# Splitting a feed-forward half between two expert stages, with its rows kept in DRAM

## The chip, the core and the metric

The kernel runs on one core of a Trainium2 chip. The metric is the device time of one execution in microseconds (us). Of the engines, PE (TensorE) multiplies, DVE, ACT and POOL work on vectors, and SP issues nearly all loads, in the order of one queue; 16 DMA engines move the data.

## The reference

Two blocks of two layers follow each other. The first takes the tokens x [256, 1024]; the second takes its output and a context ctx [256, 1024] of its own:

```python
# first block, layer i = 0, 1
h = h + (forgetting_attention if i == 0 else retention)(rms_norm(h), ...)
h = h + hier_moe(rms_norm(h), ...)         # 32 experts, two per token
# second block, layer l = 0, 1
mod, modc = silu(c) @ w_mod[l] + b_mod[l], silu(c_ctx) @ w_mod[l] + b_mod[l]   # six vectors of 1024 each
x  = x  + g1 * (mix(x, xc) @ w_out[l])     # needs the states of the context's mixer
x  = x  + g2 * swiglu(rmsnorm(x, norm2_g[l]) * (1 + sc2) + sh2, w_gu[l], w_down[l])
if l == 0:
    xc = xc + gc1 * (mix_c(xc) @ w_out[0])
    xc = xc + gc2 * swiglu(rmsnorm(xc, norm2_g[0]) * (1 + scc2) + shc2, w_gu[0], w_down[0])
```

The context's half of the second block does not depend on the first block. It is mixer, feed-forward half, and then of layer 1 only the part of the mixer that gives the states. The feed-forward half has 2816 hidden units.

## The kernel before

**Stages.** `run` (L1755) traces the main path: fox (the attention), moe(0), retention, moe(1), and then the second block's tokens. Beside each of the first four stages stands "side" work that does not depend on it. `weave` (L1737) traces a ratio R0 to R3 of side steps for each step of the main path, and what is left when the main path ends follows it (`drain`). The place in the trace becomes the place in each engine's order, save for the few pieces that a raised priority puts ahead. The side work is:

- beside fox, `early`: small vectors, then `mods(0, (0, 1))`
- beside moe(0): the context's `mixer(0, 1)`
- beside retention, `later`: `mods(0, (2,))`, the set-up of layer 1, `mods(1, (0,))`
- beside moe(1), `ctx`: the context's `ffn(0, 1)` and then `mixer(1, 1, full=False)`

**mods** (L1191) makes a third (or more) of the six modulation vectors: for each third eight loads of w_mod of 1 MB, each with four products of 128 x 512 (L1211), which appear as eight MATMUL rows since a product in f32 takes two passes.

**moe** (L846). Routing: transposes (L824), logits (L828), the choice of experts on DVE, ranks (L868 to L870), a gather of tokens by products with a one-hot matrix (L895). Then eight quads q of four experts. For each of eight k a pair of 1 MB tiles of expert_w_gu (`wload2`, L153) and 16 products of 32 rows (L956); four pairs of expert_w_down with L976; the result goes to the tokens through L986 and L988. A quad has six main steps, so 48 in all. In the last quad w_down comes as sixteen half tiles (L1010).

**ffn** (L1396) of the context, in plain f32 (mode "f"). `normed2` makes the normalised rows, transposed, as a tile xt [128, 2048] of 1 MB: scale and shift rows by products (L1241), vector work (L306 is its last step), transposes (L266). Then 11 steps r. Each has a gate half and an up half (`fs`, L416: one load of w_gu, 1 MB in rows of 1 KB, and 16 products, L430, 32 MATMUL rows) and a down part (one load of w_down of 1 MB, eight products, L1416); the down part of a step is traced after the halves of the next one.

**Weight tiles.** All loads go through one pool of six tiles of 1 MB; a load waits on SP until its tile is free, and all loads behind it on the queue wait too. At the start of moe three more tiles (`self.extra`: e0, e1, e2) lie in places that are idle then. e2 is also the place of xt in the context's halves.

Of the kernel before, what the change touches and what calls it, by code (L numbers as in the profile page):

```python
# [8 lines left out]
F32 = mybir.dt.float32  # L9
# [4 lines left out]
ALU = mybir.AluOpType  # L14
# [3 lines left out]
D, T, P = 1024, 256, 128  # L18
EPS = 1e-6
NEG = -1e30  # L20
RS = -8192.0                    # what rsqrt's scaled form carries
NE, CAP, FF = 32, 32, 512
R0, R1, R2, R3, R4 = 1.8, 0.8, 1.0, 0.88, 0.7           # steps of other work per step of the main path
AHEAD = 200                     # instructions that what the others wait for goes ahead of
TAPS = 6                        # convolution taps between other work
PIECE, WS = 512, 6              # elements per partition split at a time; pieces on chip
# [3 lines left out]
# columns of the constant array  # L30
C_ID, C_LE, C_LT, C_GE, C_ONE = 0, 128, 256, 384, 512
C_Z, C_LOW, C_UP = 640, 768, 896          # 0 where col <= row / col >= row, else NEG
C_IOTA, C_GRP, C_I8 = 1024, 1056, 1088
C_SEL, C_OFF = 1096, 1112                 # row 32 j + i, column i; rows of scales: what to add, 1 / RS
C_COS, C_SIN, C_RET = 1116, 1372, 1628         # rotary, decay
NCST = C_RET + 4 * 384

# modulation vectors: which third of the columns of w_mod, and which two of its quarters
# [4 lines left out]
def constants():  # L43
    """Tables that depend on shapes alone."""
# [35 lines left out]
class Tags:  # L80
    """A pool, some of whose tags lie in another one under other names."""
# [10 lines left out]
class Net:  # L92
    def __init__(self, tc, I, out, es):
# [10 lines left out]
        self.early, self.hold = -99, None                  # pieces of weights whose low parts GpSimd makes  # L104

# [7 lines left out]
    def bank(self):  # L113
        """One bank, from the other pool while g's are taken."""
        return self.m()[:, 0:512] if self.taken else self.g()

    def two(self, mode, apart=False):
        """Two banks."""
# [7 lines left out]
    def wt(self, name):  # L126
        """A weight tile; some lie in the places of tiles that are no longer needed."""
# [4 lines left out]
    def wload(self, src):  # L132
        """One tile of weights: rows (k p) of src on the partitions."""
# [6 lines left out]
    def wtile(self):  # L140
        """A weight tile as [P, 2, D]."""
        return self.wt("w").rearrange("p (b d) -> p b d", b=2)

    def gain(self, src, g):
        """src [D] on all partitions."""
# [3 lines left out]
    def wload2(self, src):  # L149
        """The same rows of two experts: src [2, P, 1024]."""  # L150
# [16 lines left out]
    def affine(self, o, i, scale, bias=None, eng=None):  # L167
        """o = i * scale + bias, per partition."""
# [1669 lines left out]
```

## Time and profile before

| what | value |
|---|---|
| three runs, us | 2347.91, 2349.80, 2354.22 |
| median, us | 2349.8 |
| profiled execution: span from first to last instruction, us | 2346.0 |
| mean granted clock of TensorE, share of full speed | 0.970 |
| busy share of the span: PE, DVE, ACT | 91%, 45%, 30% |
| DMA: mean rate | 293 GB/s |

The page gives no time of the profiled execution other than its span, which is 3.8 us less than the median of the runs. The stages follow from the first and last instructions of each in the timeline: fox to about 205 us, moe(0) to 770, retention to 995, moe(1) to 1632, then the second block's tokens. A view by windows gives, for each stretch, every engine's busy time, the granted clock, the busy share of the DMA engines (it can show a little over 1) and the rate in GB/s.

### The profile page before, as it was taken

What the parts mean: (1) busy time and instruction counts of PE and PEld (TensorE: products, weight loads), DVE (VectorE), ACT (ScalarE), POOL (GpSimd) and SP (SyncE); (2) the same over time, 40 slices, a digit from 0 to 9 for tenths busy, and PEclk for the clock granted to TensorE, in tenths of its full rate; (3) what the DMA queues carried; (4) which work ended last, traced back from release to release, by engine and by line L of the source; (5) the groups of instructions that cost most, each with busy time, mean ns of one, the idle gap of its engine ahead of it and who ended that gap; (6) DMA issues with size and microseconds to landing.
All of it is one profiled execution on the core that took longest, in us unless ns stands there. A gap on an engine that the chain in (4) does not pass through costs nothing. (4 is left out here: it accounts for less than half of the span.)

```text
span 2346.0 us, 32803 instructions
## 1 busy us (share of the span) xinstructions
PE 2127.2 (91%) x12844; PEld 1433.4 (61%) x12845; DVE 1060.9 (45%) x2513; ACT 695.6 (30%) x1420; POOL 172.9 (7%) x194
## 2 busy tenths in 40 slices
PE   8998899889877999989899999987998998998998
PEld 7765445344222776855444444334787997787997
DVE  6556053322101766531121221415778556777555
ACT  4353111211000434520000000012555554554554
POOL 1001000000000111010000000001212002102000
PEclk9999999999988999989999999999999999999999
DMA  8864999999999977579999999999756554555551
GB/s 257 313 245 166 350 399 392 369 399 378 379 409 384 323 281 246 203 268 382 391 398 393 399 390 390 367 356 346 256 162 202 188 190 156 187 181 171 192 185 63
DMA packets 305320, 686.64 MB, mean 293 GB/s; under 512 B 22056, under 2 KB 163784, under 8 KB 298888
## 3 DMA queue, kind: packets, MB, share of 16 engines
q1 hardware_dynamic: 305096, 684.45, 79.9%
q8 instruction: 103, 1.69, 0.3%
q14 instruction: 57, 0.47, 0.1%
q10 hardware_dynamic: 64, 0.03, 0.0%
HBM read 681.78 MB, written 2.62 MB: 292 GB/s over the span
## 5 line engine op out<-in xcount | busy, mean ns | idle before, releaser
L190 DVE TENSOR_TENSOR wl<-w,wh 128x512 fp32r<-128x512 f32 x574 | 396.3, 707 | 252.4 <-ACT wh L185 233.7
L185 ACT CAST wh<-w 128x512 fp32r<-128x512 f32 x600 | 364.3, 621 | 355.5 <-PE psm L430 111.6
L956 PE MATMUL psm<-w,xg 128*32 128x512 f32 x2048 | 319.8, 632 | 61.8 <-DMA w<-in_expert_w_gu_dram 55.0
L430 PE MATMUL psg<-xt,w 128*128 128x256 f32 x1056 | 235.8, 381 | 20.5 <-DMA w<-in_w_gu_dram 11.3
L430 PEld LDWEIGHTS psg<-xt,w 128*128 128x128 f32 x1056 | 198.0, 190 | 71.1 <-issue 38.6
L956 PEld LDWEIGHTS psm<-w,xg 128*32 128x32 f32 x2048 | 66.4, 112 | 270.6 <-issue 150.4
L430 PE MATMUL psg<-xh,wh 128*128 128x256 f32 x608 | 177.2, 291 | 3.9 <-ACT wh L185 2.4
L430 PE MATMUL psm<-xh,wh 128*128 128x256 f32 x640 | 179.9, 281 | 0.6 <-ACT ffh L1450 0.6
L430 PE MATMUL psm<-xh,wl 128*128 128x256 f32 x640 | 179.8, 281 | 0.0
L430 PE MATMUL psm<-xl,wh 128*128 128x256 f32 x640 | 179.7, 281 | 0.0
L430 PE MATMUL psg<-xh,wl 128*128 128x256 f32 x608 | 175.1, 288 | 2.4 <-DVE wl L190 2.4
L430 PE MATMUL psg<-xl,wh 128*128 128x256 f32 x608 | 173.8, 286 | 0.0
L976 PE MATMUL psm<-w,hT 128*32 128x512 f32 (+1 forms) x1152 | 156.7, 564 | 16.0 <-DMA w<-in_expert_w_down_dram 12.5
L430 PEld LDWEIGHTS psg<-xh,wh 128*128 128x128 f32 x608 | 118.1, 194 | 18.6 <-ACT wh L185 9.5
L430 PEld LDWEIGHTS psm<-xh,wh 128*128 128x128 f32 x640 | 120.7, 189 | 1.9 <-ACT ffh L1450 1.1
L430 PEld LDWEIGHTS psm<-xh,wl 128*128 128x128 f32 x640 | 120.6, 188 | 0.7
L430 PEld LDWEIGHTS psg<-xh,wl 128*128 128x128 f32 x608 | 118.0, 194 | 4.9 <-DVE wl L190 4.2
L430 PEld LDWEIGHTS psm<-xl,wh 128*128 128x128 f32 x640 | 120.8, 189 | 0.0
L430 PEld LDWEIGHTS psg<-xl,wh 128*128 128x128 f32 x608 | 117.9, 194 | 0.3 <-issue 0.2
L965 ACT ACTIVATE ha<-psm 128x512 f32<-128x512 f32 x16 | 9.6, 597 | 334.3 <-PE psm L956 334.3
L988 DVE TENSOR_TENSOR x<-x,psg 128x512 f32<-128x512 f32 (+1 forms) x72 | 45.1, 628 | 123.2 <-PE psg L986 123.0
L976 PEld LDWEIGHTS psm<-w,hT 128*32 128x32 f32 x1152 | 38.6, 111 | 93.2 <-issue 52.2
(497 smaller groups left out, 3263.9 us busy)
## 6 DMA issues: line engine op xcount, KB each, us to landing
w<-in_expert_w_gu_dram SPq DMA_DIRECT2D x256, 1024.0 KB
w<-in_expert_w_down_dram SPq DMA_DIRECT2D x112, 1024.0 KB
w<-in_w_gu_dram SPq DMA_DIRECT2D x66, 1024.0 KB
w<-in_w_mod_dram SPq DMA_DIRECT2D x48, 1024.0 KB
w<-in_w_in_dram SPq DMA_DIRECT2D x40, 1024.0 KB
w<-in_w_down_dram SPq DMA_DIRECT2D x33, 1024.0 KB
w<-in_ret_w_in_dram SPq DMA_DIRECT2D x24, 1024.0 KB
w<-in_fox_w_in_dram SPq DMA_DIRECT2D x16, 1024.0 KB
```

The source lines that it names most:

```text
L185: nc.scalar.copy(h, src)
L190: eng.tensor_tensor(l, src, h.bitcast(F32), op=ALU.subtract)
L430: self.nc.tensor.matmul(o, a, x, start=i == 0, stop=i == len(mm) - 1)
L956: nc.tensor.matmul(gu[32 * j:32 * j + 32, half * 512:(half + 1) * 512], xg[:, k, 32 * j:32 * j + 32], ws[j // 2][:, j % 2, half * 512:(hal ...
L965: nc.scalar.activation(ha, gu[:, 0:512], AF.Silu)
L976: nc.tensor.matmul(o[32 * j:32 * j + 32, :], hT[:, k, 32 * j:32 * j + 32], w(j), start=k == 0, stop=k == 3)
L988: v.tensor_tensor(o, o, ps, op=ALU.add)
```

## The change

- The modulation vectors of layer 0 are made wholly beside fox; the third that stood beside retention is gone from there.
- The context's feed-forward half is cut in two. Steps r = 0 to 3 (`SHARE = 4`) follow the mixer beside moe(0). xt is written to a DRAM buffer `keep` by a DMA on SP, and read back into its place e2 by a DMA on SP for the second part. Steps 4 to 10 stay beside moe(1). The vector g2 is made once in each part.
- One side step, the gate half of step 4, is traced ahead of moe(1), so ahead of the second routing.
- e2 is in use then, and the second moe has two extra tiles in place of three.
- The ratios are 2.4, 0.82, 0.6, 0.66 in place of 1.8, 0.8, 1.0, 0.88.

```diff
-R0, R1, R2, R3, R4 = 1.8, 0.8, 1.0, 0.88, 0.7
+R0, R1, R2, R3, R4 = 2.4, 0.82, 0.6, 0.66, 0.7
+SHARE = 4
...
     def moe(self, l):
-            self.extra = ["e0", "e1", "e2"]
+            self.extra = ["e0", "e1"] if l else ["e0", "e1", "e2"]
...
-    def ffn(self, l, i, mode, bp, b2):
+    def ffn(self, l, i, mode, bp, b2, r0=0, nr=FFN // 256, keep=None):
...
-        xin = self.normed2(l, 2, i, bp, x, mode)
+        if r0:
+            xt = bp.tile([P, 8, T], F32, tag="xt", name="xt")
+            nc.sync.dma_start(xt.rearrange("p k t -> p (k t)"), keep)
+            xin = [xt]
+        else:
+            xin = self.normed2(l, 2, i, bp, x, mode)
+        if keep is not None and not r0:
+            nc.sync.dma_start(keep, xin[0].rearrange("p k t -> p (k t)"))
...
-        nr = FFN // 256
...
-        for r in range(nr):
+        for r in range(r0, nr):
...
-            if r == 0:
+            if r == r0:
                 g2 = self.row(l, "g2", i, bp.tile([P, D], F32, tag="kt", name="g2"), mode)
...
     def run(self):
         def early():
-            yield from self.mods(0, (0, 1))
+            yield from self.mods(0)
         def later():
-            yield from self.mods(0, (2,))
             yield from self.setup_layer(1)
             yield from self.mods(1, (0,))
+        def ctx0(bp, b2):
+            yield from self.mixer(0, 1, "f", bp, b2)
+            yield from self.ffn(0, 1, "f", bp, b2, 0, SHARE, keep)
+        keep = self.dp.tile([P, 8 * T], F32, name="keep")
...
-                side = self.mixer(0, 1, "f", bp, b2)
+                side = ctx0(bp, b2)
...
             def ctx():
-                yield from self.ffn(0, 1, "f", bp, b2)
+                yield from self.ffn(0, 1, "f", bp, b2, SHARE, keep=keep)
                 yield from self.mixer(1, 1, "f", bp, b2, full=False)
             side = ctx()
+            next(side)
             self.weave(self.moe(1), side, R3)
```

Line numbers of the changed kernel are one higher up to moe, and two to eight higher behind it.

How instructions move, at three places. First PE at the second routing. Before, the last products of retention (L1165, with the split weights wh, wl and rows yh, yl) are followed by the routing's transposes of x:

```order
L1165 MATMUL psg<-wl,yh 128x512
L824 MATMUL psg<-cst,x 128x128 x8
L828 MATMUL psg<-wr,xT 128x40 x8
L868 MATMUL psg<-M,cst 128x32
L895 MATMUL psg<-oh,xn 128x128 x6
```

With the change:

```order
L1166 MATMUL psg<-wl,yh 128x512
L431 MATMUL psg<-xt,w 128x256 x16
L825 MATMUL psg<-cst,x 128x128 x8
L829 MATMUL psg<-wr,xT 128x40 x8
L869 MATMUL psg<-M,cst 128x32
```

The gate half's 16 products (L431) stand between retention's last product and the routing.

Second, SP at the same place. Before, these loads stand between retention's last weights and the last load ahead of the first wait on the routing's counts (cnti); in is w_gu of the second block, expert_w_gu of the first:

```order
L137 DMA w<-in_ret_w_out_dram 128x4x512 x7
L153 DMA w<-in_expert_w_gu_dram 128x2x1024 x7
L137 DMA w<-in_w_gu_dram 128x8x256
L1024 TENSOR_LOAD cnti
```

With the change:

```order
L138 DMA w<-in_ret_w_out_dram 128x4x512 x6
L154 DMA w<-in_expert_w_gu_dram 128x2x1024 x2
L138 DMA w<-in_w_gu_dram 128x8x256
L154 DMA w<-in_expert_w_gu_dram 128x2x1024 x5
L154 DMA w<-in_expert_w_gu_dram 128x2x1024
L1025 TENSOR_LOAD cnti
```

Eight tiles of the experts in place of seven stand ahead of the counts, and the load of w_gu two places behind retention's last.

Third, SP in moe(0) at the write of keep, with the change:

```order
L138 DMA w<-in_w_out_dram 128x4x512 x2
L154 DMA w<-in_expert_w_gu_dram 128x2x1024 x4
L138 DMA w<-in_w_gu_dram 128x8x256
L154 DMA w<-in_expert_w_gu_dram 128x2x1024 x4
L1409 DMA keep<-xt 128x2048
L138 DMA w<-in_w_gu_dram 128x8x256
```

The write of xt to keep stands behind the first load of the feed-forward half and ahead of the second; where it stands, only loads of the experts were before.

## Rows read from the trace of the kernel before

**Rows 1.** The view by windows, one row for each stage; columns stand in its head.

```profile
core 0: us, PE busy (x) PEld busy (x) DVE busy (x) ACT busy (x) POOL busy (x), PEclk, DMA share, GB/s
205.00:770.00 565.00, 476.45 (x2681) 214.94 (x2682) 141.78 (x419) 75.99 (x171) 17.76 (x30) 0.95 0.98 376
770.00:995.00 225.00, 222.22 (x1220) 174.06 (x1220) 152.32 (x321) 98.67 (x176) 28.43 (x27) 1.00 0.74 262
995.00:1632.00 637.00, 581.12 (x3145) 306.32 (x3143) 171.78 (x414) 59.94 (x136) 22.92 (x31) 0.98 0.98 371
```

**Rows 2.** The same view by 50 us: fox, moe(0), moe(1).

```profile
50.00:100.00 50.00, 48.70 (x314) 35.60 (x314) 29.11 (x75) 18.34 (x41) 0.53 (x1) 1.00 0.77 274
...
650.00:700.00 50.00, 36.59 (x198) 10.25 (x198) 2.52 (x6) 2.65 (x6) 0.00 (x0) 0.90 1.02 409
...
1250.00:1300.00 50.00, 48.33 (x252) 26.69 (x251) 10.83 (x18) 1.84 (x4) 0.76 (x2) 1.00 1.03 395
```

**Rows 3.** What PE waited for in moe(0), 217 to 770 us: total, times, longest.

```profile
PE psm L956 <- DMA w<-in_expert_w_gu_dram: 43.2, 40, 2.6
```

**Rows 4.** The same for moe(1), 1017 to 1632 us.

```profile
PE psm L956 <- DMA w<-in_expert_w_gu_dram: 11.8, 15, 1.6
```

**Rows 5.** DMA view, 730 to 770 us: rate in 40 slices of 1 us.

```profile
GB/s 410 406 401 422 410 406 401 414 418 401 390 366 351 347 346 349 350 346 348 348 347 351 346 348 353 341 347 350 347 348 347 350 346 350 346 350 345 399 388 418
```

**Rows 6.** Groups by line on PE, 0 to 205 us (fox): busy us, mean ns, idle before.

```profile
L1211 PE MATMUL psg<-w,ccol 128*32 128x512 f32 x128 | 19.1, 601 | 0.0
```

**Rows 7.** The same group, 770 to 995 us (retention).

```profile
L1211 PE MATMUL psg<-w,ccol 128*32 128x512 f32 x128 | 17.9, 604 | 0.0
```

**Rows 8.** What ACT waited for in fox, 0 to 205 us.

```profile
ACT wh L185 <- DMA w<-in_fox_w_in_dram: 10.3, 3, 6.1
```

**Rows 9.** Timeline of PE, 560 to 612 us (moe(0)): start, duration, operation.

```profile
593.08 13.97 PE L1390 MATMUL psg<-w,yT 128*128 128x512 f32 x32 [0.89 <-DMA w<-in_w_out_dram]
606.98 4.49 PE L956 MATMUL psm<-w,xg 128*32 128x512 f32 x36
```

**Rows 10.** DMA view, 570 to 612 us: rate in 40 slices of 1.05 us.

```profile
GB/s 414 406 406 410 417 410 117 23 172 339 410 355 382 390 394 423 314 398 406 396 390 402 414 400 421 410 406 406 410 417 398 414 417 254 39 27 140 312 425 324
```

**Rows 11.** Timeline of PE, 480 to 500 us (moe(0)).

```profile
485.12 1.91 PE L976 MATMUL psm<-w,hT 128*32 128x512 f32 x12 [1.57 <-DMA w<-in_expert_w_down_dram]
488.22 7.14 PE L464 MATMUL psg<-w,xt 128*128 128x256 f32 x32 [1.19 <-DMA w<-in_w_in_dram]
```

**Rows 12.** Timeline of PE at the second routing and the start of moe(1).

```profile
995.15 0.39 PE L1165 MATMUL psg<-wl,yh 128*128 128x512 f32 x1
995.38 0.60 PE L824 MATMUL psg<-cst,x 128*128 128x128 f32 x4
996.32 0.66 PE L824 MATMUL psg<-cst,x 128*128 128x128 f32 x4 [0.34 <-DVE x L725]
1004.44 0.60 PE L868 MATMUL psg<-M,cst 128*128 128x32 f32 x2 [5.54 <-DVE M L763]
1010.15 3.17 PE L956 MATMUL psm<-w,xg 128*32 128x512 f32 x16
...
1031.11 7.17 PE L430 MATMUL psg<-xt,w 128*128 128x256 f32 x32
```

**Rows 13.** Timeline of DVE at the second routing: start, duration, operation.

```profile
998.94 0.24 DVE L843 TENSOR_TENSOR rp<-rp,psg 128x80 f32<-128x80 f32 x1 [0.51 <-PE psg L828]
...
1000.59 0.42 DVE L845 SCALAR_TENSOR_TENSOR L<-rp,rs,br 128x40 f32<-128x40 f32 x2
...
1001.80 0.22 DVE L233 SCALAR_TENSOR_TENSOR rs<-rs,twh 128x1 f32<-128x1 f32 x1
```

**Rows 14.** DMA view, 1000 to 1080 us: rate in 40 slices of 2 us.

```profile
GB/s 168 308 356 207 156 8 0 0 90 426 412 418 403 404 352 116 254 416 367 70 346 322 395 370 151 412 395 412 418 396 356 335 390 393 414 424 408 393 64 295
```

**Rows 15.** DMA view, 1500 to 1540 us: rate in 40 slices of 1 us.

```profile
GB/s 397 406 397 250 74 4 35 225 406 412 401 401 414 418 406 410 414 418 397 408 391 385 309 49 2 0 0 0 180 434 381 418 389 393 414 426 410 410 340 62
```

**Rows 16.** DMA view, 1590 to 1630 us (end of moe(1)): rate in 40 slices of 1 us.

```profile
GB/s 414 414 410 401 418 406 414 401 418 414 379 358 352 346 348 350 268 61 151 361 323 309 307 368 340 342 346 356 348 348 306 365 362 343 347 352 268 94 260 399
```

## The prediction

> **What bounds the kernel now.** I read the view by windows first, a row for each stage [rows 1], since the average over the span hides that the stages have different limits. Two columns count: PE's busy time and the rate of the DMA engines. In retention PE is busy for 222.22 of 225 us at a DMA share of 0.74: every product added or removed there shows in the time. Fox is alike, with 48.70 of 50 us at a share of 0.77 [rows 2]. In moe(0) and moe(1) the share is 0.98 over the whole stage, start and routing among it. By 50 us [rows 2], moe(0)'s end moves 409 GB/s while PE is busy for only 36.59 of 50 us, and the middle of moe(1) moves 395 GB/s while PE is busy for 48.33. So both expert stages are bound by their loads, and PE has much slack in the end of moe(0) and little in moe(1). The waits say the same: PE waited 43.2 us in 40 pieces for tiles of expert_w_gu in moe(0) [rows 3], and 11.8 us in 15 pieces in moe(1) [rows 4].
>
> That is the point of the case. The change moves 12 weight tiles and the PE work that goes with them from one load-bound stage to the other. Tiles cost the same in both. What can be won is only what the expert stages lose beside the loads: stretches in which the DMA engines stand still since all weight tiles are full and PE is at something else. So I counted those in the DMA view [rows 10, 14 to 16].
>
> **The sum.** Against the span of 2346.0 us; the median of the runs lies 3.8 us higher, and the difference is then added to the median.
>
> *Modulation vectors.* The third that moves has eight loads, half of the 16 that stand in fox, where their 128 rows keep PE busy for 19.1 us [rows 6]: +9.6 us. PE is idle for 1.3 us of 50 there [rows 2], about 4 us over fox's main part; side products that need no split weights can fill some of it, and I let them fill 2.5: **+7**, between +5.6 and +9.6 as long as loads are in time. In retention the same eight loads are half of 17.9 us [rows 7], with no idle time to speak of behind them [rows 1]: **-9**. Its weaker bound is -6, PE's 2.8 us of idle time growing in their place.
>
> *The 12 tiles.* A tile of an expert moves at some 410 GB/s, 2.56 us; w_gu comes in rows of 1 KB, and the rows of 1 KB at the end of moe(0) move at 347 [rows 5], so 3.0 us. Eight w_gu and four w_down are 34.4 us, **+34.4** in moe(0) and **-34.4** in moe(1). The cover in moe(0): their PE work is 8 x 7.14 [rows 11] and, for the down parts of as many columns, 4 x 7.1 (eight products of 512 columns in place of 16 of 256), with some 7 us for the rows and the transposes of normed2, 92 us in all. PE is idle for 565 - 476 = 88.5 us there now [rows 1], and the stage grows by the loads, so some 31 us stay idle in some 602. That is 95% busy, less than the 48.33 of 50 us at which moe(1) still moves 395 GB/s [rows 2]. If that cover were gone, each step beyond it would cost its 7.1 us.
>
> *keep.* The write is 1 MB more, at 410 GB/s **+2.6**. The read falls into retention, where a quarter of the DMA time is free [rows 1]: nothing; without that cover it would be 2.6 too.
>
> *The transposed rows.* In moe(1), normed2 and the first fs are a burst of PE work with few tiles used; from 1030 to 1078 us the DMA engines slow in four places, the slices at 254 and 116, 70, 151 and 64 GB/s [rows 14], which lose 6.8 us against 410. In moe(0) the burst comes right behind the mixer's two w_out steps. No row shows it there, so I bound it: nothing, if products of experts lie well between, or two holes such as a w_out step leaves. Those are 13.97 us of PE on two tiles [rows 9], and the rates fall to 23 and then 27 GB/s behind them [rows 10], 2.5 and 3.3 us lost. I take two holes, 6, since rows, transposes and two fs stand there nearly together: **-0.8** in sum, between -6.8 and, with the write of keep holding the queue (below), much more.
>
> *The second routing.* The gate half, 7.14 us, now stands on PE ahead of the routing's transposes, which wait now only 0.34 us [rows 12]. Some of it is hidden: the logits are there at 998.94 us, but DVE multiplies them by the tokens' rstd only at 1000.59 [rows 13], 1.4 us behind the end of the operation before; rstd can be made during the gate half. And DVE makes rstd of the context's rows (twh) between the routing's operations [rows 13]; some ten such, each of which keeps the next back by some 0.08 us, are gone: 0.8. So 7.14 - 0.34 - 1.4 - 0.8 = **+4.6**, between +3 and +6.8. The DMA engines stand at 8, 0 and 0 GB/s there [rows 14] with all tiles full; one expert tile more lies ahead of the routing, as w_gu's tile is free again before it: **-2.6**, or 0 if it is not.
>
> *The end of moe(1).* normed2 of layer 1's mixer is followed by 8 us of L464 and leaves holes at 1503 to 1508 and 1522 to 1529 us [rows 15], 3.5 and 5.7 us. The burst stays, with fewer side steps around it: **-2**, between -9 and 0. The states' last steps stood inside the last quad, and slices of 268, 61 and 151 GB/s cost 1.6 us there [rows 16]; they now end before it: **-1.6**.
>
> Sum: 7 - 9 + 34.4 - 34.4 + 2.6 - 0.8 + 4.6 - 2.6 - 2 - 1.6 = **-1.8 us**, so 2348.0 on the runs' median. Its bounds that are independent make some 8 us to either side.
>
> **A rule of the clock.** The granted clock is 0.90 from 650 to 700 us, where PE waits for tiles, and 1.00 from 1250 to 1300 [rows 2]; at full speed that is the upper of the two levels, 2.4 GHz. Yet the product group at 488.22 us, straight behind waits of 1.57 and 1.19 us, took 7.14 us, and the first fs of moe(1) 7.17 [rows 11, 12]. So a thinner moe(1) costs nothing by the rows.
> The Trainium skill (TensorE: Matmul & The Clock Gate, HAM oscillation) says that waits for loads between short bursts of products let the clock fall again and again, so that each burst starts slow. By that rule, a moe(1) with a quarter less side work would run its products at 1.2 GHz in part; that is the last rival below, and by it the sum would be +26.
>
> **The rivals.**
> - *Faster: the holes go with the density (chance 0.17).* moe(1) is at 0.66 side steps for a main step in place of 0.88, and if bursts are the only cause of its holes, all 9.2 us at mixer time go, and the first burst in moe(0) leaves nothing: -1.8 - 7.2 - 6 = -15, 2335. For it: PE 48.33 of 50. Against it: the holes come from single bursts of 8 to 14 us, whose length does not change.
> - *Slower: fox waits for its weights (0.13).* All loads go through one queue and six tiles, and up to three loads of w_mod in a row now precede one of fox by the order of SP. If the queue has no slack, the eight loads cost 8 x 2.56 = 20.5 us and not 7: +11.7, **2361**. It decides where ACT's wait for fox's weights, 10.3 us in three pieces now [rows 8], comes more often than at the start. Against it: a DMA share of 0.77 [rows 2], so over 30 us of free DMA time in 150.
> - *Slower: the write of keep holds SP (0.07).* It waits for normed2's last transposes, and w_gu and the experts' tiles queue behind it. Six tiles last for 15 us; beyond that each microsecond is lost. At 10 us more: 2358. Against it: four expert tiles are ahead of it.
> - *Slower: the clock (0.05).* The granted clock is 0.90 where PE waits for tiles [rows 2]. If a thinner moe(1) let it fall to its lower level at an fs, that would take 2 x 7.14 = 14.3 us, as long as a w_out step, and leave a hole as behind that, some 4 us with the wait ahead of it; at seven of the remaining halves this is +28, **2374**. Against it: the durations above. The page's rule speaks for it.
> - *It does not do what it says:* excluded by the order of the instructions, in which four steps stand in moe(0) and the gate half ahead of the routing.
>
> **How the numbers follow.** The forecast has a chance of 0.58: 2348, itself between 2340 and 2356. About 0.3%, 7 us, is what a measurement of this kernel can tell from no change, so the borders are 2342.8 and 2356.8. Faster: the first rival, and a quarter of the forecast's case, 0.17 + 0.15 = 0.32. Slower: most of fox's and half of keep's, the clock, and a little of the forecast's: 0.10 + 0.04 + 0.05 + 0.04 = 0.23. Within: 0.45. The range leaves out the clock and the ends of the faster rival and of fox's: 2334 to 2362.
>
> **What would show it.** moe(0) should be some 43 us longer at 380 GB/s or more, with PE busy for over 550 us, and no fall of the rate over 4 us behind the write of keep. Retention should lose 9 us and fox gain 7. The transposes L825 should come 7 us behind retention's last product, and the expert's first products 5 us later than now, measured from it. moe(1), from the routing's transposes to its last product, should be some 45 us shorter: the 34.4, the holes and the tile ahead of the routing. The forecast is wrong if moe(0) grows by 50 us or more, if fox grows by more than 10, or if moe(1) at fewer side steps moves clearly more than 395 GB/s, which would mean that PE paced it.

## The result, and the profile after

The changed kernel takes 2369.8 us (median of 4 runs, 2365.24 to 2371.51), the kernel before beside it 2351.7 (4 runs): **ratio 1.0085, 95% interval 1.0068 to 1.0101**, slower by some 18 us. I had forecast 2348 and a range up to 2362. The profiled execution, the fastest of the four, has a span of 2363.5 us against 2346.0, so 17.5 us of the difference can be looked up.

First the view by windows of the changed kernel, with borders at its own stages; it answers to [rows 1].

```profile
core 0: us, PE busy (x) PEld busy (x) DVE busy (x) ACT busy (x) POOL busy (x), PEclk, DMA share, GB/s
212.00:825.00 613.00, 545.88 (x3030) 276.10 (x3031) 174.99 (x457) 78.39 (x184) 22.32 (x33) 0.99 0.97 368
825.00:1042.00 217.00, 213.17 (x1156) 172.39 (x1155) 146.72 (x318) 97.64 (x172) 28.76 (x26) 1.00 0.70 236
1042.00:1648.00 606.00, 517.67 (x2801) 246.18 (x2799) 136.64 (x349) 56.23 (x122) 18.71 (x28) 0.96 0.97 370
```

PE's work went where it should, though by less than the 92 us that I had counted for moe(0): moe(0) has some 70 us more of it and moe(1) some 63 less. The rate is the row to look at: 368 and 370 GB/s, where moe(0) had 376 and moe(1) 371 with more of the slow 1 KB rows in it.

For the sum, the stages are cut at instructions that both kernels have: the first product of the ranks (L868 before) of each routing and the last product of the combine (L986) of each expert stage.

| stretch | before | after | change | forecast |
|---|---|---|---|---|
| to the first ranks (fox) | 208.9 | 211.8 | +2.9 | +7 |
| moe(0), ranks to last combine | 561.4 | 613.3 | +51.9 | +43.0 |
| retention, to its last product | 225.1 | 217.2 | -7.9 | -9 |
| from there to the second ranks | 9.1 | 14.2 | +5.2 | +4.6 |
| moe(1), ranks to last combine | 627.4 | 591.1 | -36.3 | -47.4 |
| second block's tokens | 714.2 | 715.8 | +1.6 | 0 |

(The forecast's terms for moe(0) are 34.4, 2.6 and 6; those for moe(1) are -34.4, -2.6, -6.8, -2 and -1.6.) Fox came out 4 us better than forecast, retention and the routing within 1.1 us. The miss lies in the expert stages: +9 in one and +11 in the other. Each of these times is from one execution, and a stage varies: fox is the same in the changed kernel and in twelve kernels below and took 210.8 to 215.2 us in their profiles, and moe(0), the same in eight of them, 613.3 to 618.5.

The small terms can be seen in a few lines. The modulation vectors, groups on PE of fox and of retention (they answer to [rows 6, 7]; 8 loads are 64 rows):

```profile
L1212 PE MATMUL psg<-w,ccol 128*32 128x512 f32 x192 | 26.6, 600 | 0.0
...
L1212 PE MATMUL psg<-w,ccol 128*32 128x512 f32 x64 | 9.4, 604 | 0.0
```

Fox got 7.5 us of PE work and only 2.9 us longer; the rest filled idle time. The second routing, timeline of PE (answers to [rows 12]):

```profile
1042.35 7.07 PE L431 MATMUL psg<-xt,w 128*128 128x256 f32 x32
1049.25 1.04 PE L825 MATMUL psg<-cst,x 128*128 128x128 f32 x8
1050.64 1.98 PE L829 MATMUL psg<-wr,xT 128*128 128x40 f32 x16 [0.35 <-DVE xT L164]
1056.59 0.61 PE L869 MATMUL psg<-M,cst 128*128 128x32 f32 x2 [3.98 <-DVE M L764]
```

The gate half costs its 7 us, and the wait for the choice of experts falls from 5.54 to 3.98 us. On DVE, the product of logits and rstd now follows at once on the operation before, where 1.4 us lay between them (answers to [rows 13]):

```profile
1052.65 0.24 DVE L844 TENSOR_TENSOR rp<-rp,psg 128x80 f32<-128x80 f32 x1 [1.47 <-PE psg L829]
1052.93 0.43 DVE L846 SCALAR_TENSOR_TENSOR L<-rp,rs,br 128x40 f32<-128x40 f32 x2
```

So rstd is made under the gate half, as forecast.

The waits of PE for tiles tell where the balance went, first moe(0) from 224 us on, then moe(1) from 1069 us on (they answer to [rows 3, 4]):

```profile
PE psm L957 <- DMA w<-in_expert_w_gu_dram: 27.7, 25, 2.0
```

```profile
PE psm L957 <- DMA w<-in_expert_w_gu_dram: 58.8, 48, 2.2
```

In moe(1), PE waits 58.8 us for tiles where it waited 11.8. A stage that waits that much should be one long stretch of loads at full rate. It is not: with the change, the DMA engines stand still for a moment, again and again, and shortly after it PE waits for them.

**Loads and holes.** To see that as a number, I took the DMA view in stretches of 20 us (40 slices of 0.5 us), called a slice under 325 GB/s a hole, and counted what it lacks against 410. What is left of a stage's time is then the loads: fitted over the undisturbed stretches, 2.57 us for 1 MB in long rows and 2.98 in rows of 1 KB. With these, loads and holes give each stage's length within 2.5 us:

| stage | tiles of 1 MB (of them 1 KB rows) | us of loads | us of holes |
|---|---|---|---|
| moe(0) before | 201.6 (19.5) | 526.9 | 34.7 |
| moe(0) after | 215.4 (28.2) | 565.9 | 47.1 |
| moe(1) before | 223.6 (31.3) | 588.3 | 39.1 |
| moe(1) after | 211.6 (23.0) | 554.0 | 34.7 |

The prices of the loads were right (3.0 and 2.56 forecast). By this count, loads of 39.0 us moved into moe(0) and of 34.3 out of moe(1). The holes are what went wrong: +12.4 where I had +6, and -4.4 where I had -10.4. With them, 6.4 of the 8.9 us in moe(0) are holes, and 2.0 are loads (39.0 where I had 34.4 and 2.6). Of the 11.1 us in moe(1), 6.0 are holes, 2.6 the tile that was to be loaded ahead of the routing, and 2.4 the count leaves unexplained.

### The profile page after: what moved, and what is told of

It reads as the page before. It is cut to its first block, busy times and chain, and to the rows that moved or that the text cites. A ratio compares the mean times of both kernels' runs of the same rounds, so it can differ in the third digit from the quotient of the medians.

```text
span 2363.5 us, 32793 instructions
## 1 busy us (share of the span) xinstructions
PE 2129.7 (90%) x12848; PEld 1433.2 (61%) x12849; DVE 1056.3 (45%) x2514; ACT 695.5 (29%) x1421; POOL 173.8 (7%) x194
## 4 chain that ended last, share of the span: by engine, by line
PE 49%; DMA 10%; DVE 6%; issue 1%; ACT 1%; POOL 0%; SPq 0%; DVEq 0%; ACTq 0%; POOLq 0%
PE psm L431 10%; PE psg L431 9%; PE psg L1424 7%; DMA w<-in_expert_w_gu_dram 4%; PE psg L465 4%; PE psm L957 4%; PE psm L977 2%; DMA w<-in_w_gu_dram 2%; PE psg L1166 2%; DMA w<-in_w_down_dram 2%; PE psg L1391 2%; DMA w<-in_expert_w_down_dram 1%; PE psg L896 1%; PE psm L1439 1%; PE psm L449 1%
## 5 line engine op out<-in xcount | busy, mean ns | idle before, releaser
L957 PE MATMUL psm<-w,xg 128*32 128x512 f32 x2048 | 331.2, 631 | 89.6 <-DMA w<-in_expert_w_gu_dram 86.5
L957 PEld LDWEIGHTS psm<-w,xg 128*32 128x32 f32 x2048 | 67.6, 112 | 305.5 <-DMA w<-in_expert_w_gu_dram 149.9
L431 PE MATMUL psg<-xt,w 128*128 128x256 f32 x1056 | 236.7, 383 | 13.5 <-DMA w<-in_w_gu_dram 6.6
L431 PEld LDWEIGHTS psg<-xt,w 128*128 128x128 f32 x1056 | 198.8, 191 | 64.6 <-issue 30.6
L431 PE MATMUL psm<-xh,wh 128*128 128x256 f32 x640 | 179.9, 281 | 0.6 <-ACT ffh L1458 0.6
L431 PE MATMUL psm<-xh,wl 128*128 128x256 f32 x640 | 179.8, 281 | 0.0
L431 PE MATMUL psm<-xl,wh 128*128 128x256 f32 x640 | 179.7, 281 | 0.0
L431 PE MATMUL psg<-xh,wh 128*128 128x256 f32 x608 | 176.2, 290 | 3.4 <-ACT wh L186 1.9
L431 PE MATMUL psg<-xh,wl 128*128 128x256 f32 x608 | 175.5, 289 | 1.8 <-DVE wl L191 1.8
L431 PE MATMUL psg<-xl,wh 128*128 128x256 f32 x608 | 173.7, 286 | 0.0
L431 PEld LDWEIGHTS psg<-xh,wh 128*128 128x128 f32 x608 | 117.9, 194 | 13.5 <-ACT wh L186 6.5
L431 PEld LDWEIGHTS psm<-xh,wh 128*128 128x128 f32 x640 | 120.7, 189 | 1.9 <-ACT ffh L1458 1.1
L431 PEld LDWEIGHTS psg<-xh,wl 128*128 128x128 f32 x608 | 117.7, 194 | 5.6 <-DVE wl L191 4.6
L431 PEld LDWEIGHTS psm<-xh,wl 128*128 128x128 f32 x640 | 120.6, 188 | 0.7
L431 PEld LDWEIGHTS psm<-xl,wh 128*128 128x128 f32 x640 | 120.8, 189 | 0.0
L431 PEld LDWEIGHTS psg<-xl,wh 128*128 128x128 f32 x608 | 117.8, 194 | 0.1
L967 DVE TENSOR_TENSOR ha<-ha,psm 128x512 f32<-128x512 f32 x16 | 11.0, 687 | 232.2 <-ACT ha L966 232.2
```

The source lines that it names most:

```text
L431: self.nc.tensor.matmul(o, a, x, start=i == 0, stop=i == len(mm) - 1)
L957: nc.tensor.matmul(gu[32 * j:32 * j + 32, half * 512:(half + 1) * 512], xg[:, k, 32 * j:32 * j + 32], ws[j // 2][:, j % 2, half * 512:(hal ...
```

## The experiments

The theory after the first look: a hole is a moment in which all six tiles are full, since PE has worked for long without freeing one. Rivals: SP stands at the write of keep; the half ahead of the routing spoils what follows. All runs are compared with the kernel before on the same chip; stage times are from each run's profile, cut as above. For the changed kernel itself they are 613.3 and 591.1 us.

| kernel | moe(0) | moe(1) | median us | ratio to before, 95% |
|---|---|---|---|---|
| e1_mods | 562.1 | 626.2 | 2345.4 | 0.9986, 0.9972 to 1.0001 |
| e3_no_ahead | 613.6 | 579.0 | 2350.5 | 1.0007, 0.9994 to 1.0019 |
| e4_keep_act | 615.2 | 595.5 | 2372.6 | 1.0088, 1.0058 to 1.0118 |
| e5_after_wq | 607.0 | 571.3 | 2332.5 | 0.9923, 0.9896 to 0.9950 |
| f1_ahead68 | 613.9 | 577.9 | 2353.1 | 1.0018, 1.0008 to 1.0027 |
| f2_first_step | 615.6 | 603.6 | 2373.0 | 1.0091, 1.0074 to 1.0108 |
| f3_no_ahead_wq | 606.2 | 570.7 | 2330.0 | 0.9916, 0.9900 to 0.9933 |
| f5_na_r80 | 611.6 | 580.2 | 2346.1 | 0.9985, 0.9973 to 0.9997 |
| g1_1346 | 616.9 | 578.4 | 2355.7 | 1.0025, 1.0013 to 1.0037 |
| g2_co5 | 618.5 | 589.3 | 2366.7 | 1.0070, 1.0044 to 1.0096 |
| g0_mods_wq | 551.8 | 613.9 | 2324.6 | 0.9893, 0.9874 to 0.9912 |
| g3_best | 606.8 | 570.7 | 2331.3 | 0.9929, 0.9908 to 0.9949 |
| h1_1345 | 617.8 | 582.5 | 2361.3 | 1.0051, 1.0034 to 1.0067 |
| h2_1246 | 614.6 | 584.2 | 2359.9 | 1.0048, 1.0031 to 1.0065 |

**The modulation vectors alone** (e1_mods).

```diff
-R0, R1, R2, R3, R4 = 1.8, 0.8, 1.0, 0.88, 0.7
+R0, R1, R2, R3, R4 = 2.4, 0.8, 0.6, 0.88, 0.7
-            yield from self.mods(0, (0, 1))
+            yield from self.mods(0)
-            yield from self.mods(0, (2,))
```

> The kernel before with the third of the modulation vectors moved beside fox alone (with the ratios 2.4 and 0.6 of the change for fox and retention), nothing else. If the stage times of the changed kernel can be taken apart (fox 3.0 us longer to the first ranks, retention 7.9 us shorter), this is 4.9 us below the kernel before, some 2347. If the shorter retention came from the other edits (less small work beside it), it is within 2 us of the kernel before.

The profile has fox 2.8 us longer and retention with the routing 7.9 shorter, 226.1 in place of 234.0. The median is 3.4 us lower, with an interval that just touches no change. So this part of the change is no cause; it rather gains some 3 us, which the interval does not quite part from nothing.

**Without the gate half ahead** (e3_no_ahead).

```diff
-R0, R1, R2, R3, R4 = 2.4, 0.82, 0.6, 0.66, 0.7
+R0, R1, R2, R3, R4 = 2.4, 0.82, 0.6, 0.68, 0.7
-            next(side)
```

> The changed kernel without the gate half ahead of the second routing (ratio 0.68 in place of 0.66, so that the side work still ends in time). By the stage times the routing gets back 5.2 us, and moe(1) has one half step more, some 3 us of load: 2 us below the changed kernel. If the half ahead is what spoils moe(1) (the tiles that it leaves, the place e2 that it holds), 6 us or more below it.

18 us and more came back, beyond either expectation. By the profiles, 5.5 of them lie in the routing, but 12.1 in moe(1), which has one tile *more* to load. This run changed two things, the half and the ratio, and the next ones had to part them.

**The write of keep on another queue** (e4_keep_act).

```diff
-            nc.sync.dma_start(keep, xin[0].rearrange("p k t -> p (k t)"))
+            nc.scalar.dma_start(keep, xin[0].rearrange("p k t -> p (k t)"))
```

> The changed kernel with the write of keep issued by ACT in place of SP. Theory of the held queue: the 5.0 us hole in the DMA rate behind the second w_out step (620 to 629 us) is SP standing at the write; it falls to 2 us or less, and the time by 3 to 5 us. Theory of the bursts (PE works for 10 us and more without an expert's product, and the six tiles are full): the hole stays at 4 to 5 us, the time within 1.5 us of the changed kernel's.

The time did not fall: the ratio is 1.0088, against 1.0085 of the changed kernel. But the hole did. First the changed kernel: timeline of PE, timeline of SP, what SP waited for at the write, and the rate from 600 to 640 us in slices of 1 us:

```profile
605.70 3.64 PE L957 MATMUL psm<-w,xg 128*32 128x512 f32 x32
609.27 3.70 PE L987 MATMUL psg<-ys,sgt 128*128 128x512 f32 x8
612.81 3.60 PE L1242 MATMUL psg<-modr,cst 128*128 128x512 f32 x8
616.33 1.04 PE L957 MATMUL psm<-w,xg 128*32 128x512 f32 x2
618.12 0.66 PE L267 MATMUL psg<-cst,xn 128*128 128x128 f32 x4 [0.74 <-DVE xn L307]
621.26 1.53 PE L267 MATMUL psg<-cst,xn 128*128 128x128 f32 x12 [0.63 <-DVE xn L307]
```

```profile
607.65 2.08 SPq L154 DMA_DIRECT2D w<-in_expert_w_gu_dram  x4
623.59 0.34 SPq L1409 DMA_DIRECT2D keep<-xt  x1
```

```profile
SPq L1409 <- DVE xt L164: 13.8, 1, 13.8
```

```profile
GB/s 406 414 385 29 0 0 26 234 372 374 358 365 406 422 406 426 414 401 422 414 217 12 0 0 262 393 229 203 304 365 382 414 401 410 426 401 401 410 418 410
```

The fall at 603 us belongs to w_out. Behind it SP issues four expert tiles, some 10 us of loads, and then stands for 13.8 us at the write of keep, which needs the last rows of xt, while PE combines, makes the rows and turns them. The four tiles have landed by 620, and the rate falls. Now the same with ACT issuing the write, timelines of PE and SP and the rate, again from 600 to 640 us; all of it comes 5.0 us later in this execution:

```profile
610.70 3.64 PE L957 MATMUL psm<-w,xg 128*32 128x512 f32 x32
```

```profile
614.83 0.42 SPq L138 DMA_DIRECT2D w<-in_w_gu_dram  x1
625.65 12.46 SPq L154 DMA_DIRECT2D w<-in_expert_w_gu_dram  x4
```

```profile
GB/s 401 422 426 406 438 401 410 360 33 0 0 17 217 377 368 348 360 397 397 418 418 418 430 406 418 374 366 335 376 399 420 397 422 426 434 389 143 188 397 410
```

The fall at 608 us is that of w_out. SP goes on with w_gu at once, and this load bridges the time up to the next free tile, at 625.65: from 613 to 635 us no slice is under 335. In the 28 us from 8 us behind the last product of w_out on, the holes sum to 2.2 us, where the eight kernels with the changed kernel's moe(0) have 4.8 to 5.0. So the held queue is the cause of this hole, against the theory of the bursts. It is worth little: from the last product of w_out to the end of moe(0) this run takes 218.7 us and those eight 219.5 to 221.6, and neither moe(0) nor the whole is shorter.

**A seventh tile** (e5_after_wq), from a pool of its own during moe(0) and moe(1), as every seventh weight tile:

```diff
+        self.nw += 1
+        if self.wq and self.nw % 7 == 0:
+            return self.wq.tile([P, 2048], F32, tag="wq", name=name)
         return self.wp.tile([P, 2048], F32, tag="w", name=name)
...
+                with pool("wq0", 1) as self.wq:
                     self.weave(self.moe(0), side, R1)
                     drain(side)
```

> The changed kernel with a seventh weight tile during moe(0) and moe(1). Theory of the bursts: every hole between the routings shrinks by up to 2.6 us, the time of one tile; the holes outside the two routings sum to some 61 us, most of them under 2.6 us each, so moe(0) and moe(1) together get 25 to 40 us shorter, 2330 to 2345. Theory of the held queue or of late operands: the holes are not of full tiles, and the time falls by under 5 us.

As expected of full tiles: 19.8 us less in moe(1), 6.3 less in moe(0). (By the medians the whole falls by 37 us, by the profiled executions by 23.4; this kernel's was the slowest of its five.) In moe(1) between 1075 and 1435 us the holes sum to 0.3 us, where the changed kernel has 10.4 in as long a stretch. Over the whole of moe(1) the count of holes gives 10.3 of the 19.8 us and a tile that falls outside the stage 2.9; the remaining 6.6 us are loads that took less than their fitted prices, which the count leaves unexplained. The Trainium skill (Perfetto Trace Analysis, Optimization Strategy) says that the same gap, coming back through a stretch on the engine that should be saturated, can mean that there is not enough on-chip memory for the next tile. By that rule the rates of moe(1) pointed at the buffers; this run agrees, with 10.4 us of holes turned into 0.3 by one tile.

**Half or ratio** (f1_ahead68, f2_first_step). The first keeps the half ahead and takes 0.68:

```diff
-R0, R1, R2, R3, R4 = 2.4, 0.82, 0.6, 0.66, 0.7
+R0, R1, R2, R3, R4 = 2.4, 0.82, 0.6, 0.68, 0.7
```

> The changed kernel with 0.68 in place of 0.66 as moe(1)'s ratio; the gate half stays ahead of the routing. Theory of the places: with 0.66 a quad's side steps stand behind main steps 1, 2, 4 and 5 of six, with 0.68 behind 2, 3, 5 and 6, and the holes of about 1 us behind the side steps' products come with the first set. Then moe(1) falls from 591 to 577 to 582 us and the whole to 2355 to 2359. Theory of the half ahead: it is the half ahead that costs (its place e2, the order of the tiles), moe(1) stays at 588 to 594 and the whole at 2367 to 2372.

The second keeps 0.66 and all later places, and puts the half behind moe(1)'s first main step:

```diff
     def weave(self, main, side, ratio, more=0):
...
+            for _ in range(more):
+                next(side, None)
+            more = 0
...
-            next(side)
-            self.weave(self.moe(1), side, R3)
+            self.weave(self.moe(1), side, R3, 1)
```

> The changed kernel with 0.66 kept, the gate half not ahead of the routing but behind moe(1)'s first main step, so that all later side steps stand where they stand in the changed kernel. Theory of the places: the routing gets 5.2 us back, moe(1) has one tile more, 3 us, and keeps its holes: 590 to 596 us, the whole 2365 to 2369. Theory of the half ahead: moe(1) falls to about 579 and the whole to some 2351.

It is the ratio. (f2's moe(1) is even 8 us above its expected band, with 44.0 us of holes; its profiled execution is the slowest of its four, 6 us above their median. Why it has more holes than the changed kernel is open.) With 0.68 and the half ahead, moe(1) takes 577.9 us and the whole 2353.1; with 0.66 and no half ahead, moe(1) takes 603.6 and the whole 2373.0. A change of 0.02 in a ratio is worth some 16 us, since it decides *behind which* of a quad's six main steps the four side steps stand: 1, 2, 4, 5 with 0.66 (2, 4, 5 in the first quad), and 2, 3, 5, 6 with 0.68. Adding 0.68 up over the 48 main steps shows that from the fifth quad on they stand behind 1, 3, 4, 6, which the expectation missed; these are plain places too.

What that does shows in one pair of side steps of either kernel. The changed kernel, timeline of PE and the rate from 1160 to 1200 us in slices of 1 us:

```profile
1173.69 7.15 PE L431 MATMUL psg<-xt,w 128*128 128x256 f32 x32 [0.49 <-DMA w<-in_w_gu_dram]
1180.67 0.60 PE L970 MATMUL psg<-cst,ha 128*128 128x128 f32 x4
...
1181.95 2.77 PE L977 MATMUL psm<-w,hT 128*32 128x512 f32 x20
1184.65 2.05 PE L896 MATMUL psg<-oh,xn 128*128 128x128 f32 x16
1186.63 1.91 PE L977 MATMUL psm<-w,hT 128*32 128x512 f32 x12
1188.47 1.61 PE L896 MATMUL psg<-oh,xn 128*128 128x128 f32 x12
1189.91 7.03 PE L1424 MATMUL psg<-w,ffh 128*128 128x512 f32 x16
1196.87 3.64 PE L977 MATMUL psm<-w,hT 128*32 128x512 f32 x32
```

```profile
GB/s 254 410 315 307 381 418 410 424 337 373 378 360 414 406 410 401 426 401 410 401 426 401 410 401 426 401 410 401 422 406 406 406 430 381 406 401 332 90 205 381
```

A fs, then a main step with the gather (L896) in it, then a down part: 23.3 us of PE from 1173.69 to 1196.94, in which four expert tiles and two of its own were used, 16 us of loads. At the end all tiles are full, and the rate falls to 90: SP waited 7.9 us for the down part to free a tile (what SP waited for, 1180 to 1202 us), and its next load stands at 1196.98.

```profile
SPq L154 <- PE psg L1424: 7.9, 1, 7.9
```

```profile
1196.98 2.73 SPq L154 DMA_DIRECT2D w<-in_expert_w_gu_dram  x3
```

The same place with 0.68:

```profile
1148.07 7.15 PE L431 MATMUL psg<-xt,w 128*128 128x256 f32 x32 [1.16 <-DMA w<-in_w_gu_dram]
1155.14 2.77 PE L957 MATMUL psm<-w,xg 128*32 128x512 f32 x20
1158.25 1.91 PE L957 MATMUL psm<-w,xg 128*32 128x512 f32 x12 [0.34 <-DMA w<-in_expert_w_gu_dram]
1161.33 7.14 PE L431 MATMUL psg<-xt,w 128*128 128x256 f32 x32 [1.17 <-DMA w<-in_w_gu_dram]
1168.40 2.77 PE L957 MATMUL psm<-w,xg 128*32 128x512 f32 x20
```

```profile
GB/s 406 410 392 372 350 368 383 413 397 414 410 414 401 414 410 415 364 352 352 389 406 410 414 401 414 397 401 406 414 410 414 406 410 410 414 397 418 414 410 401
```

Between the two fs stands a main step without combine or gather. PE is done with each so early that it waits for the next tile (0.34, 1.17 us), and the rate (1140 to 1180 us) never falls below 350, that of 1 KB rows.

**Other places** (g1_1346, g2_co5, h1_1345, h2_1246). Steps at chosen places of the quad in moe(1), with the half ahead:

```diff
     def weave(self, main, side, ratio, places=()):
...
-            due += ratio
+            due += n % 6 + 1 in places if places else ratio
...
-            self.weave(self.moe(1), side, R3)
+            self.weave(self.moe(1), side, R3, (1, 3, 4, 6))
```

> The changed kernel with the gate half ahead, and moe(1)'s side steps behind main steps 1, 3, 4 and 6 of each quad. Theory of the pairs: two side steps with one main step between them, and the combine (in step 2 of the list's main steps) or the gather (in 5) in that main step, are a burst of 22 to 24 us; here the pairs 3-4 and 6-1 have a plain main step between them, as with 0.68, so moe(1) is at 576 to 583 us and the whole at 2351 to 2357. Rival: a side step behind main step 1 or 4 is bad by itself, as in 0.66 (behind 4 it stands between the last expert product and the transposes that free the next tiles); then 588 to 595 and 2364 to 2372.

g2_co5 keeps 0.66 and moves the combine of the main path:

```diff
-                    if k == 3 and left:
+                    if k == (5 if l else 3) and left:
```

> The changed kernel with 0.66, and in moe(1) the combine of the quad before put one main step later (behind k = 5 in place of k = 3), so out of the pair 1-2 and into the wider gap 2-4; the gather stays in the pair 4-5. Theory of the pairs: the holes behind the first pair of each quad go, about half of the 13 us, the whole is 2361 to 2366. Rival of the places by themselves: nothing moves, 2367 to 2372.

h1_1345 and h2_1246 are g1_1346 with (1, 3, 4, 5) and (1, 2, 4, 6):

> The changed kernel with moe(1)'s side steps behind main steps 1, 3, 4 and 5 of each quad: of the two pairs of 0.66 only that with the gather between its steps (4-5) is left, and 3-4 is a plain pair right ahead of it. Theory of the pairs: the gather is the longer of the two bursts (24 against 22 us), so this pair alone keeps most of the loss: moe(1) at 585 to 595 us, the whole at 2359 to 2372. If the pair with the combine was the cause, moe(1) is at 576 to 583, the whole at 2352 to 2357.

> The same with side steps behind 1, 2, 4 and 6: only the pair with the combine between its steps (1-2) is left, with a plain pair 6-1 right ahead of it. If each pair costs by its burst, moe(1) is at 582 to 590 us and the whole at 2356 to 2364; if the gather's pair was the cause alone, 576 to 582 and 2351 to 2356.

Holes in moe(1) in 360 us from some 20 us behind its ranks on, that is, without the routing and the mixer's end:

| places in the quad | close pairs | holes, us | moe(1), us |
|---|---|---|---|
| 1, 2, 4, 5 (0.66, as changed) | with combine, with gather | 10.4 | 591.1 |
| 2, 3, 5, 6, from the fifth quad on 1, 3, 4, 6 (0.68) | all plain | 1.2 (0.1 in the first 340 us) | 577.9 |
| 1, 3, 4, 6 | both plain | 1.7 | 578.4 |
| 1, 3, 4, 5 | with gather | 8.9 | 582.5 |
| 1, 2, 4, 6 | with combine | 7.9 | 584.2 |

Places 1 and 4, which are part of the bad set, are harmless in 1, 3, 4, 6. Either pair alone brings most of the small holes, a third to a half of the 13 us that the stage loses, and some half of the loss in the whole (1.0051 and 1.0048, between 1.0018 and 1.0085). Since g1, h1 and h2 have four side steps in each quad alike, it is their places and not their number. g1 came out as expected, h2 too; h1's moe(1) is 2.5 us under its expected band, and nothing shows the gather's pair to be the dearer of the two: moe(1) is the same in the changed kernel and in e4_keep_act, and took 591.1 and 595.5 us. g2 is inconclusive: its moe(1) is only 1.8 us shorter than the changed kernel's. The small holes left in it stand behind the gather's pair, as the theory has it.

**The ratio of moe(0)** (f5_na_r80) is e3_no_ahead with 0.80 in place of 0.82.

> The kernel without the half ahead (0.68), and 0.80 in place of 0.82 in moe(0), as before the change. Theory of the places: the 6.9 us more of holes in the mixer's part of moe(0) come from the places that 0.82 gives; they go, and moe(0) falls from 613.6 to about 606, the whole to 2342 to 2345. If those holes come from the split itself (the burst of normed2 and keep next to w_out), moe(0) stays within 2 us.

By its numbers a miss: moe(0) gets only 2.0 us shorter, which the rival had. The holes did move with the places: up to the end of w_out they fall from 38.8 to 30.1 us. But 0.80 leaves side steps over for the end of moe(0), and behind w_out the holes grow from 10.1 to 15.4. The whole is 4.4 us below e3_no_ahead by the medians, more than its expert stages explain. By the profiles it is 3.8, and 3.3 of these lie in the second block's tokens (713.6 against 716.9 us), where the two kernels are the same; over all profiles that stretch took 713.6 to 717.3 us.

**Towards a better kernel** (f3_no_ahead_wq, g0_mods_wq, g3_best). f3 is e3_no_ahead with the seventh tile of above.

> The kernel without the half ahead (0.68) with a seventh weight tile in both expert stages. Theory of the bursts: its moe(1) has 22.0 us of holes, 10.5 of them at the routing and 7.4 in the last quad but one; those longer than 2.6 us shrink by that, so moe(1) falls by 3 to 6 us; moe(0) falls by some 6 as with the seventh tile before. 2339 to 2343. If the tile's gain of 20 us in moe(1) of the changed kernel had another cause than its small holes, it comes here too: 2330 or less.

moe(1) falls by 8.3 us, moe(0) by 7.4: 2330.0, at the rival's end of what was expected. The holes in moe(1), 22.2 us, are those of e3_no_ahead, 22.1: what fell there are again the loads, 5.8 us below their fitted prices, and some 2.4 us of load that falls outside the stage. So a seventh tile does more than fill holes, and what that is stays open. g0 is e1_mods with the seventh tile, so *without* the split:

> The kernel before with the modulation vectors beside fox and a seventh weight tile in both expert stages, without the split of the feed-forward half. If the split gains nothing, as the stage times say, it is as fast as the split kernel without the half ahead and with the seventh tile (2330.0): 2327 to 2335. If the split pays as soon as the holes are small, it is 6 us or more slower, 2336 and up.

2324.6 us: **the fastest of all, 1.1% below the kernel before** and 5.4 below the split one with the same tile. (That one ran on another chip, and the intervals of the two ratios just overlap.) View by windows of g0_mods_wq, borders at its stages:

```profile
212.00:764.00 552.00, 470.84 (x2682) 214.75 (x2683) 138.59 (x391) 72.76 (x169) 17.75 (x30) 0.96 1.00 385
764.00:995.00 231.00, 218.70 (x1183) 177.11 (x1181) 154.80 (x377) 105.90 (x192) 28.39 (x27) 0.98 0.67 227
995.00:1609.00 614.00, 570.82 (x3118) 303.28 (x3117) 165.64 (x355) 53.34 (x121) 23.06 (x30) 0.99 0.99 380
```

Both expert stages move 9 GB/s more than before at the same work [rows 1]. Last, g3_best is f3 with chosen places and w_out in two side steps:

```diff
-            self.weave(self.moe(0), side, R1)
+            self.weave(self.moe(0), side, R1, (2, 3, 4, 5, 6))
-            self.weave(self.moe(1), side, R3)
+            self.weave(self.moe(1), side, R3, (2, 3, 5, 6))
...
                         self.residual(xs, ps[h][b], g1[:, h * 512:(h + 1) * 512], b, mode == "r" and b and h)
+                if mode == "f" and k0:
+                    yield
             yield
```

> The split without the half ahead, with the seventh tile, side steps behind 2, 3, 5 and 6 in moe(1) and behind all but the first in moe(0), and each w_out step of the context's mixer cut into two side steps of 7 us. Theory of the bursts: the two w_out holes (2.2 and 4.2 us) and some of the normed2 hole go, moe(0) falls by 5 to 8 us against the same kernel without these: 2321 to 2326. If moe(0)'s holes have other causes, 2328 to 2332.

A miss: 2331.3, moe(0) 606.8 as in f3. The holes up to the end of w_out are few (26.5 us), those behind it 15.2; with all steps but one taken, each burst stands next to another, which may be why; no run shows it.

## Why the prediction was wrong

- **What bounds the kernel** was right: loads in both expert stages, PE in fox and retention. The loads cost what was forecast.
- **Modulation vectors**: -2 forecast, -5.0 measured, by +2.9 in fox and -7.9 in retention. Fox had more idle time to fill (7.5 us of work for 2.9 us); but its 210.8 to 215.2 us in other executions leave room for +1.9 to +6.3.
- **The second routing**: +4.6 forecast, +5.2 measured. The tile more ahead of it did not give 2.6 us: the holes there are some 11 us with the change, some 10 before.
- **keep** costs the 1 MB of its write, and SP does stand at it: 13.8 us, and a hole of 3.7 us ahead of the write. So the rival of the held queue was right in its mechanism, but the hole is no cause of the miss, since e4_keep_act is without it and as slow. I had 6 us for two bursts behind w_out; 3.7 of what came is this stand, so that size was right in part by luck.
- **The step that failed** is the sum over the holes of the expert stages, which put new holes in moe(1) at nothing. I listed the holes of the kernel before, let some go with the density ("the burst stays, with fewer side steps around it"), and allowed new ones only for normed2. For the rest I leaned on averages: PE 95% busy in moe(0) against 48.33 of 50 us in moe(1), so cover enough. But an average of PE says nothing of six tiles. Of the holes that I let go in moe(1), those of normed2 and the first fs did (some 8 us, 1030 to 1080 us before). But 0.66 brought a hole behind seven of the nine pairs from 1080 to 1440 us, 10.4 us, where the kernel before has 5.2 in the same window. With 0.68 (f1_ahead68) they are gone, moe(1) is 13 us shorter and the whole some 16. Most of the loss hangs on that one number: with 0.68 the change is 1.0018 times before, 3.6 us and inside the range that I gave, and without the half ahead 1.0007. That was in front of me: the places of the steps could be counted from the ratio and the order of PE.
- **moe(0)** was 9 us too long by the same step: 6.9 us of its holes are in the mixer's part, where the work is the same and only 0.80 became 0.82 (f5_na_r80 takes them back, and pays behind w_out), and 5.4 behind it, where I had 6.
- **The signs**: moe(0) grew by 51.9 us, over the 50 that I had named as a refutation, at 368 GB/s and not 380, with PE busy for 545.88 us and not over 550.
- **The rivals**: the faster one (holes go with the density) is what 0.68 shows for the small holes, 1.2 us in 360, but not for the mixer's hole, one of 9.0 us in the changed kernel and of 5.5 with 0.68. The clock did fall: over moe(1) the granted clock is 0.96 where it was 0.98, and behind waits of PE it fell for moments. From 1169 to 1173 us it was 0.57, and 12 rows of expert products (L957) took 3.48 us, which take 1.91 above; the loads went on at 381 GB/s. Yet the whole fs and down parts took 7.0 to 7.2 us (7.15 and 7.03 above), save one fs of 8.15 us, and where the rate fell to 90 the granted clock was 1.00. So the rows of the fs were right but for 1 us, and the clock is not the cause of these holes. The view by windows and the timeline of PE:

```profile
1180.00:1200.00 20.00, 19.99 (x122) 9.83 (x123) 8.04 (x15) 2.06 (x5) 0.76 (x2) 1.00 0.97 377
1280.00:1290.00 10.00, 7.66 (x26) 3.31 (x27) 0.00 (x0) 0.00 (x0) 0.00 (x0) 0.66 1.04 391
```

```profile
1286.95 8.15 PE L431 MATMUL psg<-xt,w 128*128 128x256 f32 x32
```

Two slips in the prediction's working change nothing: the idle time left in moe(0) comes to 33 us of 602 and not 31, and the price of the clock's rival to 2376 and not 2374.

That the split itself gains nothing was right as a statement on loads, and two pairs of runs that differ else only in the expert stages' ratios agree: without the half ahead it is 5.1 us slower by the medians (e3_no_ahead against e1_mods, on one chip), and with a seventh tile 5.4 (f3_no_ahead_wq against g0_mods_wq, on two), though the intervals of each pair overlap a little. Not tried was the split with other numbers of steps.

## What to carry to other kernels

A stage that is bound by its loads loses time when its buffers are full, or when the queue stands at something else, so look for the moments at which the transfer rate falls and ask how long the consumer has worked without freeing a buffer, and what the queue waited for; mean busy shares cannot show it. Side work that is woven in by a ratio lands at fixed places of the main loop: count which main steps lie between two side steps, and keep those with long extra work (a gather, a combine) out of the narrow gaps. One more buffer was worth 20 us and more in each of the three kernels that got it (20.8 between e1_mods and g0_mods_wq, by the medians), more than any shift of work between stages, and should be tried before such a shift.

## What I had not expected of the hardware

With tiles always free, one queue kept the mean rate at 400 to 414 GB/s for tiles of long rows and at some 350 for rows of 1 KB: 2.57 and 2.98 us for 1 MB, fitted over the stretches without holes of moe(0) and of moe(1) in both kernels, 350 us and more of each, and within 0.1 us the same in all four. With a seventh tile the loads of moe(1) took some 3 to 6 us less than these prices (554.2 us by them in f3_no_ahead_wq, with 22.2 of holes, in a stage of 570.7).
